# Hybrid attention encoder: in the first layer, both groups of sliding attention between differential heads 1 and 2, and an output projection that begins with their rows

## The chip, the cores and the metric

The kernel runs on one core of a Trainium2 chip. The metric is the device time of one execution in microseconds. The engines are TensorE (PE for its matmuls, PEld for its weight loads), VectorE (DVE), ScalarE (ACT), GpSimd (POOL) and SyncE (SP), which issues every DMA of this kernel.

## The reference, cut to what matters

Two sequences are encoded, a prompt of 16 + 1024 tokens and a sample of 16 + 512 tokens (the 16 are shared meta tokens). Each of two layers projects the normalised tokens, computes two kinds of attention on them, multiplies by gates, and projects back.

```python
def layer(x, ...):
    h = rmsnorm(x, pre_g)
    proj = einsum('bld,de->ble', h, w_in)            # aq ak av ag bq bk bv bg
    oa = window_gqa_attention(aq, ak, av, sink) * silu(ag)   # 8 query heads, 2 key heads
    ob = diff_attention(bq, bk, bv, lam, ...) * silu(bg)     # 4 heads, two softmaxes each
    o = einsum('ble,ed->bld', concatenate([oa, ob], -1), w_out)
    return x + rmsnorm(o, post_g)

def diff_attention(q, k, v, lam, lambda_init, subln_g):   # over all keys
    p = softmax(einsum('bqhcd,bkhcd->bhcqk', q, k) * scale)
    a = p[:, :, 0] - lam * p[:, :, 1]
    return rmsnorm(einsum('bhqk,bkhe->bqhe', a, v), subln_g) * (1 - lambda_init)
```

The sliding attention looks at a band of 128 keys to each side, at the meta tokens and at a sink.

## The kernel before, in words

A recording layer takes down every operation with what it reads and writes (so every instruction of the profile carries line 448, and tiles are told apart by name), and a planner then orders them: `Recorder.schedule` walks through a model of the engines, and each engine takes the ready operation with the lowest priority number. The number of an operation is its place in the written program, less a boost of its kind and less a base of its stage. Each engine runs its instructions in the planned order; a wait on the chip does not change it.

A layer has six attention units: four differential heads (`attn_b`, heads 0 to 3; the tuple `UNITS` calls them 0 to 3) and two groups of sliding attention (`attn_a`, groups 0 and 1; `UNITS` calls them 4 and 5). Each unit does the prompt and then the sample. The weight columns of the input projection that a unit needs (4 blocks of 128 for a differential head, 6 for group 0 with the shared keys and values, 4 for group 1) are projected while the unit before it runs:

```python
for u in range(6):
    nc.base = BASE_A[l][u]
    order[u][1](l)                                   # the attention of this unit
    if u + 1 < 6:
        es = [(e, None, 0) for e in order[u + 1][0]]  # the projection for the next
        for grp in GROUPS[1 if len(es) == 4 else 2]:
            inproj(l, *[es[i] for i in grp])
outproj(l)
```

So "fill" on PE, the dense products that stand between the pieces of an attention unit, comes from the input projection for the next unit, and for the last unit from the output projection. Tiles: `ps_d` are the two PSUM buffers of all dense products, `ps_s` the scores (one buffer), `ps_t` transposes, `ps_o` attention outputs; `pp` holds probabilities, `at` their transposes, `kk`, `qq`, `vv` the keys, queries and values, `whl` the split weights, `slot` the large activation buffers (16 of them). A product `ps_d<-slot,whl` belongs to the input projection, one with `whl,slot` (or `whl,at`, `kk`, `vv` in the place of `whl`) to the output projection. After a differential head or a sliding group, its output `og` goes to the HBM tensor `MX`, from where `load_mix` fetches it for the output projection.

The output projection has two passes over the 1024 rows of MX. `first` multiplies half `FH[l]` of them for all tokens and keeps the result; `second` multiplies the other half, chunk of tokens by chunk, and adds. Half 0 are the rows of the sliding groups, half 1 those of the differential heads. The order of the steps is written out: `b01234` is `first` for all five chunks, `f01` fetches the residual, `S01` is `second` for chunks 0 and 1, `p` are the norm and the residual, `n` the transposes for the next layer, `s4 s2 s3` the rest of `second`.

Of the kernel before, what the change touches and what calls it, by code (L numbers as in the profile page):

```python
# [55 lines left out]
GROUPS = (((0, 1), (2, 3)), ((0, 1), (2, 3)), ((0, 1), (2, 3), (4, 5)))  # L56
COMB = ((1, 1, 1, 1), (1, 1, 1, 1))
BASE = ({'f': 400, 'p': 100, 's': -100, 'S': 0, 'b': 800, 'g': -50}, {'f': 0, 'S': 400, 'l': 1000})
BASE_A = ((-200, 1500, 1500, -200, 200, 400), (0, 0, 0, 0, 1500, 300))
FH = (1, 1)  # L60
UNITS = ((0, 1, 2, 3, 4, 5), (0, 1, 2, 3, 4, 5))


def even_tiles(t0, n, m):
# [475 lines left out]
def hymba_kernel(ctx, tc, xT, xr, w_in, w_out, rope, masks, pre_g, post_g, sub_g, sink_b, sink_m, lam_in, yo):  # L540
# [244 lines left out]
    def load_w(src, pool=None, pri=0):  # L785
        nc.boost = BOOST_W + pri * 100000
        nc.extra = [after[0]] if pool and after else []
        raw = (p_p if pri or pool and after else wraw_p)([128, 1024])
        dma(raw, src)
        nc.boost = BOOST_W  # L790
        w = (pool or whl_p)([128, 2, 8, 128], F32R)
        rv = raw.rearrange("p (a c) -> p a c", a=8)
        nc.any_copy(w[:, 0], rv)
        nc.any_tt(w[:, 1], rv, f32(w[:, 0]), ALU.subtract)
        nc.extra = []
        nc.boost = 0
        return w
# [502 lines left out]
    def load_mix(l, ci, half, small=False):  # L1300
        nc.boost = BOOST_M
        his, los = [], []
        k = 2 if small else 4
        n = sum(m for _, m in OCH[ci])
        for r0 in range(4 * half, 4 * half + 4, k):
            if ci == 4:
                hi, lo = [at_p([128, 4, n], F32R) for _ in range(2)]
            else:
                hi, lo = [p_p([128, 2, CN], F32R) for _ in range(2)] if small else pair(F32R)
            o = 0  # L1310
            nc.extra = [after[0]] if small else []
            for (t0, m) in OCH[ci]:
                dma(lo[:, :, o:o + m], SC[l]["MX"][r0:r0 + k, :, t0:t0 + m].rearrange("e p t -> p e t"))
                o += m
            nc.extra = []
            nc.any_copy(hi[:, :, 0:n], f32(lo[:, :, 0:n]))
            nc.any_tt(lo[:, :, 0:n], f32(lo[:, :, 0:n]), f32(hi[:, :, 0:n]), ALU.subtract)
            his.append(hi)
            los.append(lo)
        nc.boost = 0  # L1320
        return rows(his, k), rows(los, k)
# [4 lines left out]
    def outproj(l):  # L1326
# [18 lines left out]
        def first(*cs_):  # L1345
            for ci in cs_:
                mix[ci] = load_mix(l, ci, FH[l])
                if ci < 4:
                    part[ci] = halves([128, 3, 512])
            for dp in range(4):  # L1350
                w = load_w(w_out[l, FH[l], dp])
                u, c0 = dp // 2, 256 * (dp % 2)
# [16 lines left out]
        def load(ci):  # L1369
            mix[ci, 1] = load_mix(l, ci, 1 - FH[l], ci == 3 and l > 0)  # L1370

        def second(*cs_, keep=True):
# [9 lines left out]
            def get(dp):  # L1382
                if dp not in kept:
                    w = load_w(w_out[l, 1 - FH[l], dp], (None, None, k_p, v_p)[dp] if keep else None)
                    if keep:
# [139 lines left out]
    for l in range(NL):  # L1525
        order = [units[u] for u in UNITS[l]]
        es = [(e, pool, START.get(f"w{i}", 0) if l == 0 else 0)
# [3 lines left out]
        for u in range(6):  # L1531
            nc.stream = "attn"
            nc.base = BASE_A[l][u]
            order[u][1](l)
# [63 lines left out]
```

## Time and profile before

| | |
|---|---|
| median of 3 runs | 1920.6 us (1920.0 to 1920.7) |
| the profiled execution | 1922.3 us, of which the span from first to last instruction is 1920.5 us |
| PE busy with matmuls | 1840.4 us, 96% |
| PE busy with weight loads | 1772.5 us, 92% |
| VectorE, ScalarE, GpSimd busy | 1487.8, 1028.0, 267.7 us |
| mean granted TensorE clock | 0.99 of full speed |

Busy time counts a matmul from its start to its modelled end, and matmuls overlap, so that 96% says that PE has seldom nothing at all in work, not that it runs at its peak.

### The profile page before, as it was taken

How to read it: one execution, taken by the hardware profiler on the slowest of the kernel's cores; microseconds unless marked ns; L12 is line 12 of the kernel's file. 1: busy time of each engine (PE TensorE's matmuls, PEld its weight loads, DVE VectorE, ACT ScalarE, POOL GpSimd, SP SyncE). 2: the span in 40 equal slices, each digit the busy share in tenths (PEclk: the TensorE clock that was granted, in tenths of full speed). 3: DMA queues.
4: the chain of work that ended last, by engine and by line, in shares of the span. 5: the costliest groups of instructions: out<-in, count | busy, mean ns of one | idle time of the engine just before them, and what ended most of it. 6: DMA issues, size and time to landing. Idle time of an engine off the chain costs nothing.

```text
span 1920.5 us, 35745 instructions
## 1 busy us (share of the span) xinstructions
PE 1840.4 (96%) x12400; PEld 1772.5 (92%) x12400; DVE 1487.8 (77%) x3353; ACT 1028.0 (54%) x2458; POOL 267.7 (14%) x521
## 2 busy tenths in 40 slices
PE   7999999999999998998799999999999999989998
PEld 7999999999999898898699999999999999889998
DVE  7577787888796887676987387887968859879777
ACT  8345454465554666565664255454546537658642
POOL 2011111212121110010220021111211111101101
PEclk9999999999999998999899999999999999999999
DMA  8444453634545665655454444445453475684374
GB/s 252 133 107 125 132 135 110 165 84 131 155 101 148 158 163 135 148 140 147 154 182 115 134 119 136 130 118 156 109 167 107 125 174 127 157 221 115 84 238 150
DMA packets 296498, 273.04 MB, mean 142 GB/s; under 512 B 100822, under 2 KB 259670, under 8 KB 296190
## 3 DMA queue, kind: packets, MB, share of 16 engines
q1 hardware_dynamic: 296318, 270.76, 51.0%
q8 instruction: 99, 1.62, 0.4%
q14 instruction: 81, 0.66, 0.1%
HBM read 149.19 MB, written 96.01 MB: 128 GB/s over the span
## 4 chain that ended last, share of the span: by engine, by line
PE 72%; DMA 10%; DVE 9%; issue 3%; ACT 3%; SPq 3%; POOL 1%; DVEq 0%; POOLq 0%; ACTq 0%
PE ps_d L448 44%; PE ps_s L448 10%; PE ps_o L448 9%; PE ps_t L448 9%; SPq L448 3%; DVE at L448 2%; DVE pp L448 2%; DVE slot L448 2%; DMA slot<-MX 1%; ACT pp L448 1%; DMA kk<-AK 1%; DVE whl L448 1%; DVE sm L448 1%; DVE og L448 1%; DMA wraw<-in_w_in_dram 1%
## 5 line engine op out<-in xcount | busy, mean ns | idle before, releaser
L448 PE MATMUL ps_d<-slot,whl 128*128 128x392 f32 (+2 forms) x4560 | 939.9, 346 | 16.2 <-ACT slot L448 6.9
L448 PEld LDWEIGHTS ps_d<-slot,whl 128*128 128x128 f32 x4560 | 782.6, 189 | 23.8 <-ACT slot L448 6.8
L448 PE MATMUL ps_s<-kk,qq 128*128 128x264 f32 (+9 forms) x1496 | 284.5, 319 | 21.4 <-DMA qq<-qq 6.5
L448 PE MATMUL ps_o<-at,vv 128*128 128x256 f32 (+6 forms) x1368 | 284.7, 306 | 5.8 <-DVE og L448 2.6
L448 ACT ACTIVATE at<-ps_t 128x256 fp32r<-128x256 f32 (+10 forms) x426 | 184.7, 440 | 195.9 <-PE ps_t L448 170.9
L448 DVE TENSOR_TENSOR at<-ps_t,at 128x256 fp32r<-128x256 f32 (+6 forms) x472 | 225.3, 481 | 78.7 <-ACT at L448 63.9
L448 PE MATMUL ps_d<-whl,slot 128*128 128x256 f32 x1800 | 263.7, 291 | 16.2 <-DVE slot L448 10.9
L448 ACT ACTIVATE pp<-ps_s,sm 116x1040 f32<-116x1040 f32 (+4 forms) x208 | 204.0, 981 | 131.9 <-DVE sm L448 120.7
L448 PEld LDWEIGHTS ps_s<-kk,qq 128*128 128x128 f32 (+4 forms) x1496 | 226.3, 184 | 45.2 <-issue 9.4
L448 PEld LDWEIGHTS ps_d<-whl,slot 128*128 128x128 f32 x1800 | 238.3, 194 | 22.8 <-DVE slot L448 13.3
L448 ACT ACTIVATE pp<-pp,sm 128x336 f32<-128x336 f32 (+6 forms) x347 | 207.5, 611 | 91.8 <-DVE sm L448 88.8
L448 DVE TENSOR_REDUCE sm<-ps_s 116x1 f32<-116x1040 f32 (+4 forms) x208 | 218.5, 1051 | 47.4 <-PE ps_s L448 46.0
L448 PEld LDWEIGHTS ps_o<-at,vv 128*128 128x128 f32 (+1 forms) x1368 | 213.8, 189 | 13.2 <-DVE at L448 3.7
L448 PE MATMUL ps_t<-ident,pp 128*128 128x128 f32 (+6 forms) x1280 | 206.3, 268 | 3.6 <-ACT pp L448 2.0
L448 PEld LDWEIGHTS ps_t<-ident,pp 128*128 128x128 f32 (+6 forms) x1280 | 151.1, 137 | 14.2 <-ACT pp L448 2.6
L448 POOL TENSOR_TENSOR pad<-pp,pad 128x64 fp32r<-128x64 f32 (+5 forms) x148 | 54.4, 372 | 756.4 <-ACT pad L448 410.2
L448 POOL TENSOR_TENSOR sm<-sm 128x2 f32<-128x2 f32 (+3 forms) x112 | 51.0, 456 | 466.8 <-DVE sm L448 439.3
L448 DVE CUSTOM_DVE_ANT_0 pp<-ps_s,mk,nsinks 128x336 f32<-128x336 f32 (+2 forms) x192 | 97.2, 527 | 19.5 <-PE ps_s L448 17.8
L448 POOL TENSOR_TENSOR sm<-sm,mhalf 128x1 f32<-128x1 f32 (+6 forms) x107 | 82.5, 783 | 165.5 <-DVE sm L448 162.5
L448 ACT ACTIVATE og<-ps_o 64x128 f32<-64x128 f32 (+4 forms) x248 | 66.7, 287 | 45.2 <-PE ps_o L448 29.2
L448 ACT ACTIVATE ru<-ps_d 128x392 f32<-128x392 f32 (+5 forms) x101 | 49.0, 486 | 73.3 <-PE ps_d L448 62.5
L448 DVE CAST at<-ps_t 128x256 fp32r<-128x256 f32 (+9 forms) x142 | 69.7, 491 | 18.7 <-PE ps_t L448 16.3
(157 smaller groups left out, 2115.6 us busy)
## 6 DMA issues: line engine op xcount, KB each, us to landing
wraw<-in_w_in_dram SPq DMA_DIRECT2D x46, 512.0 KB
qq<-qq SPq DMA_DIRECT2D x144, 128.0 KB
BS<-st SPq DMA_DIRECT2D x64, 196.0 KB
qq<-AQ SPq DMA_DIRECT2D x96, 128.0 KB
gl<-GT SPq DMA_DIRECT2D x72, 128.0 KB
MX<-og SPq DMA_DIRECT2D x72, 128.0 KB
slot<-MX SPq DMA_DIRECT2D x11, 768.0 KB
kk<-BS SPq DMA_DIRECT2D x8, 1040.0 KB
```

Source lines behind the costliest of these rows:

```text
L448: fn(*[_real(a) for a in args], **{k: _real(a) for k, a in kw.items()})
```

## The change

Five numbers and tuples change; no operation is added or taken away. In the first layer the units run in the order head 0, head 1, group 0, group 1, head 2, head 3 (before: heads 0 to 3, then the groups). `BASE_A` goes by place in this order: the last unit's base is 1900 in place of 400. `FH` of the first layer turns from 1 to 0: `first` takes the rows of the sliding groups, `second` those of the differential heads.

```diff
-BASE_A = ((-200, 1500, 1500, -200, 200, 400), (0, 0, 0, 0, 1500, 300))
-FH = (1, 1)
-UNITS = ((0, 1, 2, 3, 4, 5), (0, 1, 2, 3, 4, 5))
+BASE_A = ((-200, 1500, 1500, -200, 200, 1900), (0, 0, 0, 0, 1500, 300))
+FH = (0, 1)
+UNITS = ((0,1,4,5,2,3), (0,1,2,3,4,5))
```

Both programs hold 12400 matmuls. The first 1267 stand in the same order in both, and so do all from the 6511th on, counted from the start of the program; the second layer's order is the same on every engine. What differs lies between.

First place: PE in the prompt part of sliding group 1. Before, products of the output projection (`whl,slot`) stand between its pieces:

```order
L448 MATMUL ps_s<-kk,qq 128x336 x2
L448 MATMUL ps_d<-whl,slot 128x256 x18
L448 MATMUL ps_o<-at,vv 128x256 x4
L448 MATMUL ps_t<-ident,pad 80x128 x4
L448 MATMUL ps_d<-whl,slot 128x256 x6
L448 MATMUL ps_t<-ident,pp 128x128 x4
L448 MATMUL ps_d<-whl,slot 128x256 x3
L448 MATMUL ps_o<-at,vv 128x256 x2
L448 MATMUL ps_t<-ident,pp 128x128 x4
L448 MATMUL ps_o<-at,vv 128x512
```

In the changed kernel the fill of this unit is the input projection for head 2 (`slot,whl`), and in one stretch, of which the middle is shown, there is none:

```order
L448 MATMUL ps_d<-slot,whl 128x392 x9
L448 MATMUL ps_t<-ident,pp 64x128 x4
L448 MATMUL ps_s<-kk,qq 128x336 x4
L448 MATMUL ps_t<-ident,pad 80x128 x4
L448 MATMUL ps_s<-kk,qq 128x336 x2
L448 MATMUL ps_o<-at,vv 128x512 x2
L448 MATMUL ps_o<-at,vv 128x256 x5
L448 MATMUL ps_o<-at,kk 128x256
L448 MATMUL ps_o<-at,vv 128x512
L448 MATMUL ps_s<-kk,qq 128x336 x6
L448 MATMUL ps_t<-ident,pp 128x128 x8
L448 MATMUL ps_t<-ident,pp 64x128 x4
```

From the row behind the first one here on, 91 matmuls (the 3396th to the 3486th) follow each other without one into `ps_d`.

Second place: PE in the sample part of head 3. Before, its fill is the input projection for group 0:

```order
L448 MATMUL ps_s<-kk,qq 106x264 x4
L448 MATMUL ps_t<-ident,og 116x128 x2
L448 MATMUL ps_t<-ident,og 112x128
L448 MATMUL ps_d<-slot,whl 128x384 x12
L448 MATMUL ps_s<-kk,qq 106x264 x4
L448 MATMUL ps_d<-slot,whl 128x384 x3
```

In the changed kernel this is the last unit of the layer, its fill is `S01`, and between chunk 0 and chunk 1 of it stand 43 matmuls (the 5695th to the 5737th) with none, of which these are the last:

```order
L448 MATMUL ps_s<-kk,qq 106x264 x4
L448 MATMUL ps_o<-at,vv 128x212 x3
L448 MATMUL ps_t<-ident,pad 80x106 x2
L448 MATMUL ps_o<-at,vv 128x212 x4
L448 MATMUL ps_s<-kk,qq 106x264 x4
L448 MATMUL ps_t<-ident,og 106x128 x2
L448 MATMUL ps_s<-kk,qq 106x264 x4
L448 MATMUL ps_t<-ident,sm 128x106 x2
L448 MATMUL ps_s<-kk,qq 104x264 x4
L448 MATMUL ps_d<-whl,slot 128x256 x15
```

Third place: PE where the layer's last attention output is made. Before, the last `ps_o` matmul of group 1 is the 6027th, and the transposes for the next layer (`ps_t<-ident,slot`) follow soon:

```order
L448 MATMUL ps_d<-whl,slot 128x256 x3
L448 MATMUL ps_o<-at,vv 128x512
L448 MATMUL ps_d<-whl,at 80x256 x3
L448 MATMUL ps_d<-whl,slot 128x256 x57
L448 MATMUL ps_t<-ident,slot 128x128 x8
```

In the changed kernel the last `ps_o` matmul, of head 3, is the 5856th, and the rest of `S01` stands behind it:

```order
L448 MATMUL ps_o<-at,vv 128x316
L448 MATMUL ps_d<-whl,slot 128x256 x9
L448 MATMUL ps_t<-ident,og 106x128 x2
L448 MATMUL ps_t<-ident,og 104x128
L448 MATMUL ps_d<-whl,slot 128x256 x21
L448 MATMUL ps_t<-ident,sm 128x106 x2
L448 MATMUL ps_t<-ident,sm 128x104
L448 MATMUL ps_d<-whl,slot 128x256 x93
```

So the layer's attention ends 171 matmuls earlier in PE's order, and 159 matmuls, up to the 6016th, need nothing of the last group of tokens.

## Rows read from the trace of the kernel before

**Rows 1.** The page, part 1: busy us, share of the span, instructions.
```profile
PE 1840.4 (96%) x12400; PEld 1772.5 (92%) x12400; DVE 1487.8 (77%) x3353; ACT 1028.0 (54%) x2458; POOL 267.7 (14%) x521
```

**Rows 2.** Windows: heads 1 to 3, both groups, hand-over; second layer's group 0.
```profile
core 0: us, PE busy (x) PEld busy (x) DVE busy (x) ACT busy (x) POOL busy (x), PEclk, DMA share, GB/s
233.32:621.70 388.38, 384.54 (x2527) 370.86 (x2525) 319.80 (x620) 194.65 (x409) 65.06 (x140) 1.00 0.47 128
621.70:940.45 318.75, 295.14 (x2119) 280.43 (x2120) 246.79 (x731) 195.64 (x567) 33.40 (x69) 0.97 0.57 148
940.45:1021.16 80.71, 69.15 (x486) 66.48 (x485) 70.24 (x133) 51.98 (x120) 20.52 (x22) 0.92 0.52 170
1578.46:1717.01 138.55, 129.97 (x820) 121.62 (x819) 115.29 (x331) 90.93 (x254) 14.34 (x27) 1.00 0.64 164
```

**Rows 3.** The chain that ended last: start us, us, what.
```profile
975.91 13.11 PE ps_d L448 x111
...
1060.78 11.27 PE ps_d L448 x63
```

**Rows 4.** Timeline of PE: start us, us, instructions; transposes.
```profile
619.95 0.71 PE L448 MATMUL ps_t<-ident,pp 106*128 106x106 f32 x6
...
622.89 0.44 PE L448 MATMUL ps_t<-ident,pp 106*128 106x106 f32 x3
```

**Rows 5.** Groups of PE by form, 621.70 to 940.45: count, busy us, mean ns.
```profile
L448 PE MATMUL ps_d<-whl,slot 128*128 128x256 f32 x879 | 128.1, 291 | 6.8 <-DVE slot L448 4.1 <-ACT slot L448 2.7
L448 PE MATMUL ps_d<-slot,whl 128*128 128x392 f32 x183 | 41.1, 350 | 0.0
L448 PE MATMUL ps_d<-slot,whl 128*128 128x384 f32 x192 | 40.2, 343 | 0.1
L448 PE MATMUL ps_s<-kk,qq 128*128 128x336 f32 x128 | 28.4, 337 | 7.5 <-DMA qq<-qq 5.6 <-DVE sm L448 1.9
```

**Rows 6.** Windows: group 0's prompt, a fed stretch, the second layer's group 0.
```profile
621.70:722.55 100.85, 96.78 (x611) 90.70 (x611) 84.15 (x243) 64.86 (x179) 14.74 (x27) 1.00 0.66 166
...
428.10:431.50 3.40, 3.40 (x30) 3.29 (x30) 2.36 (x6) 2.74 (x6) 0.00 (x0) 1.00 0.00 0
1600.00:1640.00 40.00, 39.54 (x259) 36.73 (x258) 38.59 (x115) 32.56 (x95) 6.64 (x11) 1.00 0.51 129
```

**Rows 7.** Timeline of PE where group 0's sample part begins.
```profile
729.96 0.40 PE L448 MATMUL ps_s<-kk,qq 128*128 128x336 f32 x1
733.90 0.62 PE L448 MATMUL ps_s<-kk,qq 128*128 128x336 f32 x1 [3.54 <-DMA qq<-qq]
736.38 2.05 PE L448 MATMUL ps_s<-kk,qq 128*128 128x336 f32 x6 [1.86 <-DVE sm L448]
```

**Rows 8.** Windows before, in and after the slow clock around that stall.
```profile
724.00:731.00 7.00, 6.09 (x35) 5.37 (x33) 5.49 (x14) 2.98 (x9) 0.35 (x1) 1.00 0.95 252
731.20:741.30 10.10, 5.54 (x22) 5.15 (x23) 6.94 (x23) 7.37 (x21) 0.86 (x3) 0.50 0.73 204
741.40:748.40 7.00, 7.00 (x58) 6.78 (x57) 6.14 (x23) 4.49 (x14) 0.32 (x1) 1.00 0.25 50
```

**Rows 9.** Groups of DVE by form, 621.70 to 940.45: count, busy us, mean ns.
```profile
L448 DVE CUSTOM_DVE_ANT_0 pp<-ps_s,mk,nsinks 128x336 f32<-128x336 f32 x64 | 34.8, 560 | 3.5 <-PE ps_s L448 2.5 <-PE ps_t L448 0.5
L448 DVE TENSOR_TENSOR at<-ps_t,at 128x512 fp32r<-128x512 f32 x40 | 27.5, 687 | 9.5 <-ACT at L448 5.3 <-PE ps_o L448 2.7 <-ACT sm L448 0.8
L448 DVE SCALAR_TENSOR_TENSOR og<-ps_o,og 64x128 f32<-64x128 f32 x92 | 24.4, 284 | 8.9 <-ACT og L448 8.1
L448 DVE TENSOR_TENSOR whl<-wraw,whl 128x1024 fp32r<-128x1024 f32 x13 | 15.8, 1218 | 4.0 <-ACT whl L448 3.9
```

**Rows 10.** Timeline of PE in the hand-over to the second layer.
```profile
943.04 3.09 PE L448 MATMUL ps_d<-whl,slot 128*128 128x256 f32 x24 [0.78 <-DVE slot L448]
949.30 4.64 PE L448 MATMUL ps_d<-whl,slot 128*128 128x256 f32 x24 [3.17 <-DVE slot L448]
...
956.54 1.33 PE L448 MATMUL ps_t<-ident,slot 128*128 128x128 f32 x5 [2.28 <-ACT slot L448]
959.75 0.80 PE L448 MATMUL ps_d<-whl,slot 128*128 128x256 f32 x2 [1.88 <-ACT slot L448]
962.10 4.42 PE L448 MATMUL ps_d<-whl,slot 128*128 128x256 f32 x19 [1.55 <-DVE slot L448]
```

**Rows 11.** The chain, 850 to 1000: start us, us, what; a load of MX and its split.
```profile
862.89 6.38 DMA slot<-MX
869.29 1.49 ACT slot L448
870.81 1.77 DVE slot L448
```

## The prediction

> **What bounds the kernel now.** I read the page's busy times first, then windows by stage, then the order of the two programs. TensorE has matmuls in work for 96% of the span, VectorE works 77% of it [rows 1]. As no operation is added or taken away, only the time in which PE is not fed can change, and only between the places where the two orders are the same: from the 1386th matmul before (the first scores of head 1, at 233.32 us, the 1387th after) to the 6511th, at 1021.16 us. That is 787.84 us in three stages [rows 2]: heads 1 to 3 take 388.38, the two sliding groups 318.75, and the hand-over behind the last attention output 80.71.
>
> Busy time hides most of the loss, since a matmul that waits in the pipeline still counts. So I count what the matmuls of a stage take when PE is fed. In fed runs, 111 products of 256 columns take 13.11 us, 118 ns each, and 63 of 392 columns take 11.27 us, 179 ns each [rows 3]: at a full clock of 2.4 GHz both are columns/2.4 ns and 11 to 16 ns more, and I take 13 for all widths. A transpose adds 0.09 us ((0.71 - 0.44)/3) [rows 4]; I take 0.1. Counting each stage's forms at these prices (the largest of the sliding stage are in [rows 5]) gives:
> heads 1 to 3, 375.3 us of fed work in 388.4, a factor of 1.035; the groups, 276.8 in 318.75, 1.152; the hand-over, 62.0 in 80.7, 1.30. In the second layer, group 0 alone, with the input projection as fill, has 123.9 in 138.55, 1.118. The loss sits in the sliding stage (42 us) and in the hand-over (19 us), heads lose 13.
>
> What ends the waits there: in the groups the queries' load, late by 3.54 us and then by a chain of scores [rows 7]; in the hand-over VectorE and ScalarE, which add, norm, split and transpose for PE [rows 10] while VectorE is busy 70.24 of 80.71 us [rows 2].
>
> By the Trainium skill ("Perfetto Trace Analysis", "Identifying the Most-Contended Engine") a matmul's busy share is no good measure of how far PE is from its limit. The trace agrees: by busy time these stages have 39 us to give back (388.38 - 384.54, 318.75 - 295.14, 80.71 - 69.15), by the count of fed work 74.
>
> **The change, part by part.** Fed work of the changed order, counted in the same way, with VectorE's instructions of each part at what their forms add to its busy time in the trace (the largest in [rows 9]):
>
> Head 1, to the 2263rd matmul: 130.6 us of PE. Its fill is the projection for group 0, as head 3 had before. At 1.035: 135.2.
>
> Groups 0 and 1, 2263rd to 3966th: 256.0 us. Their fill is now wholly the input projection (products of 384 and 392 columns), no longer the products of `first`. The nearest row is the prompt part of group 0 before, 92.0 us of fed work in 100.85, 1.096 [rows 6]; second layer's group 0, where loads of MX run beside it, has 1.118, the whole stage before 1.152. I take 1.096 for all but one stretch, since here no MX loads run beside the groups: 244.5 x 1.096 = 268.0. The stretch is the 91 bare matmuls: 11.5 us of PE, beside which the order has 24.2 us of VectorE (8 of the wide mask-and-minimum instructions at 0.56, 5 wide and 3 half-wide remainders at 0.69, 10 merges of 0.28, a weight split of 1.22, the rest rotations and splits for head 2's projection, which hold the two `ps_d` buffers) and 15.6 of ScalarE. The trace of before shows no such stretch: its longest without a dense product has some 30 matmuls and lies at 428.1, where PE is busy for all of 3.40 us [rows 6]. Bounds: 11.5 if VectorE's work spreads over the neighbours, and 24.2/0.87 = 27.8 if VectorE keeps the share that it has in the hand-over. I take VectorE at the share that it reaches where it is the bound, 38.59 of 40 [rows 6]: 25.1. Sum for the groups 293.1.
>
> Heads 2 and 3, 3966th to 5857th: 245.3 us. Fill is the projection for head 3, then `first` and `S01`. VectorE has 201.4 us there, less in proportion than before, so 1.035 holds: 240.6 x 1.035 = 249.0. The rest is the second bare stretch: 4.7 us of PE, 8.7 of VectorE, because chunk 1 of `S01` needs the last prompt outputs of this very head. Bounds 4.7 and 10.0; I take 8.7/0.965 = 9.0.
>
> Behind the last attention output, 5857th to 6016th: 18.9 us of products that are ready, x 1.035 = 19.6. This is the gain of the edit to `FH` and `UNITS`: before, the last output's way through MX (6.38 us of load, 1.49 and 1.77 of splitting [rows 11]) lay half bare in front of `s2` and `s3` [rows 10].
>
> The hand-over, 6016th to 6511th: 63.2 us of PE but 76.6 of VectorE, against 71.4 counted so for before, since both halves of the residual work (`p0`, `p1`) now stand behind the attention. VectorE bounds it, so the 80.7 us of before scale: 80.7 x 76.6/71.4 = 86.6. Bounds: 76.6/0.965 = 79.4, and 86.6 + 6.4 if the load of chunk 2, which stands only 20 matmuls ahead of its use, is waited for bare.
>
> Sum: 135.2 + 268.0 + 25.1 + 249.0 + 9.0 + 19.6 + 86.6 = 792.5 against 787.8, 4.7 us more. The profiled execution took 1922.3 us, its span 1920.5, the median of the runs is 1920.6; the difference is put on the median: **1925 us**.
>
> **A second price for the bare stretches.** Around the stall at 730 the granted clock fell from 1.00 to 0.50, that is to 1.2 GHz, for 10.1 us, in which PE was busy 5.54, and came back after dense products [rows 8]. If that follows both bare stretches, up to half of 10.1 us is lost twice, 10.1 us in all. I leave it out of the sum, because in the bare stretches matmuls keep coming, where at 730 PE stood still for 3.54 and then 1.86 us [rows 7].
>
> The Trainium skill ("TensorE: Matmul & The Clock Gate", "Why this matters for your kernels") says that idle gaps between bursts of matmuls bring the lower clock back, so it speaks against this order. By it the sum would be 802.6; the trace agrees for the stall at 730, no run here shows a bare stretch of this kind.
>
> **The rivals.**
> *The groups run freely (faster).* Place: the sliding groups, in which MX loads no longer stand in front of the queries. For it: the worst wait before is such a load [rows 7], with DMA at 0.95 [rows 8]. Against it: group 0's prompt had no MX loads either and stood at 1.096, as VectorE has 84.15 of its 100.85 us [rows 6]. At the heads' 1.035 the groups cost 253.1 in place of 268.0: 1910. It decides from a factor of 1.06 down, where the sum is 9 us smaller.
> *Nothing measurable.* The work is the same and the loss only moves: VectorE takes the hand-over at 0.965 (79.4) and the bare stretches stay: 785.3, 1918.
> *The clock.* Both bare stretches halve it: 10.1 more, 1935.
>
> **How the numbers follow.** A difference of 0.2%, 3.8 us, is about what a measurement of this kernel can tell. Chances: the forecast 0.46 (own range 1920 to 1932), the groups freely 0.27, nothing measurable 0.16, the clock 0.11. Faster than 1916.8: nearly all of the second and a little of the third, 0.27. Slower than 1924.4: seven tenths of the first and all of the fourth, with a trace of the third, 0.45. Within: 0.28. With all low bounds together the sum would be about 40 us smaller, with all high ones (1.152 for the groups, bare 27.8 and 10.0, the clock, the load) 34 us larger; they will not fall together. The range is 1908 to 1940, from the rival on the faster side to just past the clock's.
>
> **What would show it.** Windows of the changed trace between its own places: head 1 in about 135 us; the groups in 293, with PE fed 1.1 times outside one stretch of some 25 us in group 1's prompt, in which VectorE is near 0.95 and `ps_d` does not appear; heads 2 and 3 in 258 with a second hole of 4 us; 20 us of pure products behind the last `ps_o`; then 87 us with VectorE above 0.85. From the 6511th matmul on, 899 us as before. It is wrong if the groups take under 280 us, if the bare stretch takes less than 17 us, if the hand-over ends in under 80, or if loads of MX hold up head 2, which I price at nothing because its queries and keys are issued well ahead.

## The result, and the profile after

The changed kernel takes 1949.05 us (median of four runs, 1947.1 to 1951.2) where the kernel before, run beside it, takes 1920.65. The ratio is 1.0133, 95% interval 1.0116 to 1.0150: slower by some 26 us (the two medians by themselves are 28 apart), on the side that was forecast, and outside the range of 1908 to 1940. The profiled execution took 1948.07 us.

The first rows are part 1 of the page, then windows of the changed kernel: the whole stretch in which the orders differ, then head 1; group 0, prompt and sample; group 1, prompt and sample; head 2; head 3; the products behind the last attention output; the hand-over; at last the two bare stretches.

```profile
PE 1853.8 (95%) x12400; PEld 1776.0 (91%) x12400; DVE 1481.2 (76%) x3345; ACT 1030.6 (53%) x2471; POOL 273.4 (14%) x516
```

```profile
core 0: us, PE busy (x) PEld busy (x) DVE busy (x) ACT busy (x) POOL busy (x), PEclk, DMA share, GB/s
234.14:1044.12 809.98, 759.10 (x5124) 718.56 (x5125) 629.87 (x1474) 442.45 (x1102) 125.65 (x226) 0.98 0.49 136
...
234.14:376.00 141.86, 134.59 (x877) 129.15 (x877) 110.30 (x220) 67.27 (x145) 24.76 (x47) 1.00 0.45 122
376.00:470.31 94.31, 89.40 (x554) 82.78 (x555) 78.75 (x236) 60.40 (x175) 15.12 (x29) 0.98 0.56 138
470.31:527.91 57.60, 52.01 (x317) 49.52 (x316) 36.01 (x120) 28.56 (x88) 3.33 (x8) 0.97 0.59 152
527.91:627.02 99.11, 87.87 (x509) 79.77 (x510) 80.89 (x238) 56.26 (x167) 10.58 (x21) 0.93 0.56 136
627.02:679.50 52.48, 51.90 (x327) 48.99 (x327) 38.40 (x122) 30.31 (x91) 5.77 (x9) 1.00 0.55 147
...
679.50:819.08 139.58, 131.87 (x914) 126.11 (x913) 107.91 (x197) 69.52 (x143) 20.25 (x43) 0.99 0.48 137
819.08:948.54 129.46, 123.80 (x979) 118.64 (x980) 93.97 (x183) 72.18 (x159) 19.50 (x40) 0.99 0.36 106
...
948.54:967.65 19.11, 19.11 (x162) 18.83 (x160) 12.02 (x28) 8.38 (x17) 4.24 (x9) 1.00 0.78 235
967.65:1044.12 76.47, 68.56 (x497) 64.78 (x496) 71.62 (x134) 49.56 (x117) 22.09 (x21) 0.98 0.48 163
...
573.79:600.52 26.73, 18.63 (x92) 15.12 (x92) 24.93 (x70) 15.98 (x46) 3.56 (x5) 0.81 0.51 122
921.95:933.21 11.26, 7.07 (x46) 5.45 (x45) 8.85 (x21) 7.40 (x19) 1.49 (x3) 0.93 0.39 120
```

The same stretch in the kernel before, then its heads 1, 2 and 3:

```profile
233.32:1021.16 787.84, 748.83 (x5128) 717.77 (x5127) 636.83 (x1482) 442.26 (x1095) 118.98 (x231) 0.98 0.52 140
233.32:363.98 130.66, 130.37 (x866) 126.89 (x864) 110.21 (x212) 62.21 (x129) 21.29 (x49) 1.00 0.47 128
363.98:487.82 123.84, 122.59 (x809) 117.64 (x808) 101.31 (x196) 65.24 (x137) 21.41 (x45) 1.00 0.47 130
487.82:621.70 133.88, 131.58 (x859) 126.33 (x857) 108.28 (x213) 67.19 (x144) 22.35 (x46) 1.00 0.47 126
```

The stretch takes 809.98 us against the 787.84 before, 22.1 more. Of the other 3.6 us by which the two profiled executions differ, 2.8 lie in the second layer, whose order is the same in both. VectorE is busy for less time than before in the stretch, PE for 10 us more, and the mean granted clock is 0.98 of full speed in both: neither more work nor a lower clock is the difference. PE's weight loads stand idle for 70.1 us of the stretch before (787.84 - 717.77) and for 91.4 after, 21 more: PE is fed worse.

The price of fed work from the prediction tells where it is. Elapsed time less fed work, in us, by stage (for the kernel before, heads 1, 2, 3 as they stood then; "tail" is all behind the last attention output, up to the 6511th matmul; matmuls are counted from 0):

| | head 1 | head 2 | head 3 | groups | tail | sum |
|---|---|---|---|---|---|---|
| before | 2.6 | 4.6 | 5.8 | 42.1 | 18.7 | 73.8 |
| changed | 11.2 | 13.3 | 10.4 | 47.6 | 13.5 | 96.0 |

Each line is one execution; e7 below, which has the changed kernel's order and nearly all of its work, gave a sum of 98.0, so a sum is good to some 2 or 3 us.

The tail gives 5 us back, the groups lose 5 more, and the three heads, the best stages of the kernel before, lose 22 more, 6.6 of it in the bare stretch of head 3 (11.26 us for 4.7 of fed work). PE's waits there are in front of the attention's own pieces. These are rows of the timelines of PE, ACT, DVE and SP in head 1 of the changed kernel (start us, us, instructions, and in brackets the idle time before them and what ended it):

```profile
258.58 0.42 PE L448 MATMUL ps_t<-ident,pp 116*128 116x116 f32 x2 [1.57 <-DVE st L448]
...
257.09 0.65 ACT L448 ACTIVATE st<-ps_t 96x256 fp32r<-96x256 f32 x2 [2.07 <-DMA AK<-st]
...
257.77 0.75 DVE L448 TENSOR_TENSOR st<-ps_t,st 96x256 fp32r<-96x256 f32 x2 [4.06 <-ACT st L448]
...
254.42 1.06 SPq L448 DMA_DIRECT2D AK<-st  x2
```

Read from the bottom: SP issues the last stores of a projected block of keys out of `st` until 255.48. There is one buffer `st`, so ScalarE's split of the next block stands until these have landed, 2.07 us; VectorE's half of that split stands behind it, 4.06 us; and the transposes of head 1's probabilities stand behind both on PE. Fill there was, but later in PE's queue. In head 2 it is the same buffer:

```profile
694.69 1.22 PE L448 MATMUL ps_s<-kk,qq 128*116 128x264 f32 x6 [1.35 <-ACT pp L448]
...
690.40 0.85 ACT L448 ACTIVATE st<-ru 128x768 fp32r<-128x768 f32 x1 [2.32 <-DMA BS<-st]
...
684.24 4.97 SPq L448 DMA_DIRECT2D BS<-st  x8
...
692.26 2.18 SPq L448 DMA_DIRECT2D BS<-st  x4
```

SP takes 4.97 us to issue the eight stores of one block; ScalarE stands for 2.32 in front of `st`, and the softmax that would free the one score buffer stands behind it. The next four stores follow at 692.26, when `st` has been filled again.

### The profile page after: what moved, and what is told of

Read it like the earlier page. It is cut to its first block, busy times and chain, and to the rows that moved or that the text cites. A ratio compares the mean times of both kernels' runs of the same rounds, so it can differ in the third digit from the quotient of the medians.

```text
span 1946.3 us, 35786 instructions
## 1 busy us (share of the span) xinstructions
PE 1853.8 (95%) x12400; PEld 1776.0 (91%) x12400; DVE 1481.2 (76%) x3345; ACT 1030.6 (53%) x2471; POOL 273.4 (14%) x516
## 5 line engine op out<-in xcount | busy, mean ns | idle before, releaser
L448 PE MATMUL ps_s<-kk,qq 128*128 128x264 f32 (+10 forms) x1496 | 287.6, 321 | 24.7 <-ACT pp L448 7.6
L448 ACT ACTIVATE at<-ps_t 128x256 fp32r<-128x256 f32 (+11 forms) x430 | 185.6, 438 | 215.6 <-PE ps_t L448 183.8
L448 PE MATMUL ps_o<-at,vv 128*128 128x256 f32 (+7 forms) x1368 | 286.1, 307 | 10.7 <-DVE at L448 6.4
L448 DVE TENSOR_TENSOR at<-ps_t,at 128x256 fp32r<-128x256 f32 (+6 forms) x472 | 225.6, 482 | 86.0 <-ACT at L448 65.5
L448 ACT ACTIVATE pp<-pp,sm 128x336 f32<-128x336 f32 (+7 forms) x344 | 205.8, 611 | 99.6 <-DVE sm L448 95.7
L448 PEld LDWEIGHTS ps_o<-at,vv 128*128 128x128 f32 (+1 forms) x1368 | 215.0, 190 | 21.8 <-DVE at L448 12.2
L448 PE MATMUL ps_t<-ident,pp 128*128 128x128 f32 (+5 forms) x1280 | 205.5, 269 | 10.2 <-ACT pp L448 3.7
L448 PEld LDWEIGHTS ps_t<-ident,pp 128*128 128x128 f32 (+5 forms) x1280 | 151.5, 137 | 22.9 <-ACT pp L448 4.5
L448 POOL TENSOR_TENSOR pad<-pp,pad 128x64 fp32r<-128x64 f32 (+4 forms) x140 | 51.9, 373 | 735.8 <-ACT pad L448 413.4
L448 POOL TENSOR_TENSOR sm<-sm 128x2 f32<-128x2 f32 (+2 forms) x112 | 52.1, 466 | 486.6 <-DVE sm L448 472.6
L448 DVE CUSTOM_DVE_ANT_0 pp<-ps_s,mk,nsinks 128x336 f32<-128x336 f32 (+2 forms) x192 | 97.5, 528 | 15.2 <-PE ps_s L448 14.1
L448 POOL TENSOR_TENSOR sm<-sm,mhalf 128x1 f32<-128x1 f32 (+7 forms) x107 | 84.8, 802 | 169.7 <-DVE sm L448 163.1
L448 ACT ACTIVATE ru<-slot 128x512 f32<-128x512 f32 (+1 forms) x82 | 51.3, 626 | 56.4 <-DVE slot L448 53.3
```

Source lines behind the costliest of these rows:

```text
L448: fn(*[_real(a) for a in args], **{k: _real(a) for k, a in kw.items()})
```

## The experiments

### Is it the bases? (e1 to e4)

Theory P says that the bases suit the old places, theory S that the order of the units costs this much whatever the bases.

```diff
 changed     BASE_A = ((-200,  1500, 1500, -200,  200, 1900),
+e1          BASE_A = ((-200,  1500, 1500, -200,  200,  400),
+e2          BASE_A = ((-200,  1500,  200,  400, 1500, 1900),
+e3          BASE_A = ((-200,  -200,  200,  400, 1500, 1900),
+e4          BASE_A = ((-200,  -200, 1500, -200,  200, 1900),
```

> The changed kernel with one edit undone: the base of the last unit is 400 again, so that S01 is not held back behind head 3. Theory P (the loss comes from bases that do not suit the units at their new places): head 3 alone changes; its bare stretch grows from 43 to 65 matmuls with 13.6 us of VectorE, which costs 3 us more than the 11.25 us of the changed kernel: 1952. Theory S (the loss comes from the order of the units, whatever the bases): the same, 1949 to 1952. This run separates the base of 1900 from the rest: were it the cause, the time would fall to about 1930.

> The changed kernel with the bases that the units had before carried to their new places: group 0 gets 200, group 1 gets 400, head 2 gets 1500 (changed kernel: 1500, -200, 200); head 1 keeps 1500, head 3 keeps 1900. Theory P: head 2 loses the 4.6 us that it lost before instead of 13.3, the bare stretch in group 1's prompt (62 matmuls in place of 91) costs 10.5 in place of 15.2, head 3's (25 in place of 43) 3 us less: 1949 - 8.7 - 4.7 - 3 = 1933. Theory S: the bare stretches alone shrink, head 2 keeps its loss of 12 us beside the splits of MX: 1949 - 7.7 = 1941.

> As the kernel with the bases by unit, and head 1, whose fill is now the projection for group 0, gets -200, the base that head 3 had with this fill before. Theory P: head 1 loses 5.9 us in place of 11.2, head 2 4.6 in place of 13.3; but the order has bare stretches of 62 matmuls in group 0's prompt (7.2 us of PE, 15.2 of VectorE, about 9 us lost) and of 99 in group 1's (26.4 of VectorE, about 1 us more than now), head 3's shrinks (3 us less): 1949 - 5.3 - 8.7 + 9 + 1 - 3 = 1942. Theory S: heads 1 and 2 keep their losses, 1949 + 9 + 1 - 3 = 1956.

> The changed kernel with the base of head 1 alone turned from 1500 to -200, so that the projection for group 0 goes ahead of the head's attention as it did in head 3 before. Theory P: head 1 loses 5.9 us in place of 11.2; the order of all later units shifts, and a bare stretch of 111 matmuls (13.3 us of PE, 18.3 of VectorE) stands in head 3 in place of the one of 43, which loses 6 to 8 us more than none: 1949 - 5.3 + 1 = 1945. Theory S: head 1 keeps 11 us of loss, 1950. Head 1's own stage decides: about 142 us of elapsed time for 135.8 of fed work by P, 147 by S.

Measured, as ratios to the kernel before beside them: e1 1.0152 (1.0124 to 1.0179), e2 1.0115 (1.0081 to 1.0148), e3 1.0145 (1.0119 to 1.0170), e4 1.0149 (1.0114 to 1.0184). None is told from the changed kernel's 1.0133. Put on 1920.65 us, e2 (1943) and e4 (1949) come out where theory S had them, e3 (1949) halfway between P and S. By stages:

| | head 1 | head 2 | head 3 | groups | tail | sum |
|---|---|---|---|---|---|---|
| e1 | 10.6 | 12.2 | 14.1 | 50.5 | 18.0 | 105.4 |
| e2 | 11.3 | 8.7 | 12.4 | 47.0 | 18.2 | 97.6 |
| e3 | 7.4 | 5.5 | 10.7 | 58.1 | 19.0 | 100.7 |
| e4 | 6.4 | 9.6 | 23.3 | 51.1 | 16.6 | 107.0 |

Stage by stage, P is right: head 1 with -200 loses 6.4 and 7.4 in place of 11.2, head 2 with 1500 loses 8.7 and 5.5 in place of 13.3. In the sum it is wrong: what a base gives to one stage is lost in another, in e1, e3 and e4 above all as longer or new bare stretches, and the tail's gain of 5 us is gone in e1, e2 and e3.

### Is it VectorE's load? (e5 to e7)

e5 and e6 cut the same 100 rotation instructions short in both kernels, at the moment at which the planned order is written out, so that no order changes; e7 cuts the split of MX.

```diff
+SMALL = tuple(range(0, 10)) + tuple(range(14, 26))
...
+def small(x):                       # on the operands of a marked VectorE instruction
+    if isinstance(x, View) and x.shape[-1] > 8:
+        return x[tuple([slice(None)] * (len(x.shape) - 1) + [slice(0, 8)])]
+    return x
...
+nc.small = l == 0 and e in SMALL    # e5, e6: rw<-ps_d and ru<-ru,rw of the rotations
+nc.small = l == 0 and half == FH[0] and ci < 4    # e7: slot<-slot in load_mix
```

> The kernel before, its order of instructions unchanged on every engine, with 100 VectorE instructions of the first layer's rotations cut to 8 columns each (rw<-ps_d and ru<-ru,rw of the projections for heads 1 to 3 and both groups; the queries and keys are then wrong beyond these columns): 45.1 us less of VectorE, 12.3 beside head 0, 11.3 beside head 1, 4.3 beside head 2, 8.6 beside head 3, 8.6 beside group 0. Theory V (VectorE's load under the fill is what the attention chain waits for): the heads here lose only 2.6 to 5.8 us each and give back 1 us each, group 0 some 4: 1921 - 7 = 1914. Theory O (what costs is where the order places chains without fill, VectorE's load is beside the point): 1918 to 1920.

> The changed kernel, its order unchanged, with the same 100 VectorE instructions cut to 8 columns: 45.1 us less of VectorE, 9.3 beside head 0, 8.6 beside head 1, 8.6 beside group 0, 9.3 beside group 1's prompt (2.5 of it in the bare stretch), 6.3 beside head 2, 3.0 beside group 1's sample. Theory V: head 1 gives back 4 of its 11.2 us of loss, the groups 5 and 6, head 2 3: 1949 - 18 = 1931, and the distance to the kernel before with the same cut falls from 28 us to 17. Theory O: at most the 2.5 us of the bare stretch and a few more, 1944, and the distance stays at 25 or more.

> The changed kernel, its order unchanged, with the four VectorE instructions of 1.75 us that split the sliding rows of MX for the output projection cut to 8 columns (6.9 us less of VectorE, all in head 2's prompt; the low parts of these rows are then wrong). Theory V: head 2's prompt, 94.9 us for 82.7 of fed work, falls by 3 to 5 us, to 91, and the time to 1945. Theory O: 0 to 1 us, 1948 to 1949.

Measured: e5 1.0011 (0.9996 to 1.0026), e6 1.0092 (1.0070 to 1.0114), e7 1.0126 (1.0104 to 1.0148). The cut took less than was counted on: the 100 instructions fell from 53 us to 17.5, 35 us in place of 45, and as instructions overlap, VectorE's busy time fell by 30 us in e5 and 31 in e6 (part 1 of their pages, against 1487.8 and 1481.2):

```profile
PE 1840.0 (96%) x12400; PEld 1773.0 (92%) x12400; DVE 1457.5 (76%) x3353; ACT 1026.5 (53%) x2458; POOL 262.5 (14%) x521
...
PE 1852.2 (95%) x12400; PEld 1776.3 (91%) x12400; DVE 1449.9 (75%) x3345; ACT 1029.8 (53%) x2471; POOL 268.8 (14%) x516
```

| | head 1 | head 2 | head 3 | groups | tail | sum |
|---|---|---|---|---|---|---|
| e5 (before, cut) | 2.8 | 4.7 | 5.5 | 44.8 | 19.2 | 76.9 |
| e6 (changed, cut) | 9.5 | 14.9 | 11.0 | 44.9 | 15.8 | 96.1 |
| e7 (changed, less split) | 10.9 | 13.4 | 10.7 | 48.9 | 14.1 | 98.0 |

The kernel before makes nothing of it. The changed kernel's ratio falls by 0.41%, 8 us, about halfway between theories O and V, and the distance from 1.33% to 1.0092/1.0011, 0.81%. But the two ratios of the changed kernel carry some 0.2% each, and the profiled execution of e6, the slowest of its four, shows no gain in the stretch: head 1 and the groups lose 4 us less, head 2, head 3 and the tail 4 more. So the worth of this cut by itself is not shown. The split of MX is no cause: head 2 loses 13.4 us without its time. And the bare stretch in group 1's prompt, out of which the cut took 3 us of VectorE (24.93 to 21.90), is 3.6 us shorter, with VectorE busy for 95% of it and a clock of 0.93 in place of 0.81; the window of e6:

```profile
571.23:594.39 23.16, 15.29 (x92) 12.41 (x91) 21.90 (x66) 15.52 (x44) 3.40 (x5) 0.93 0.52 123
```

### Another place for the groups (e8)

```diff
-UNITS = ((0,1,4,5,2,3), (0,1,2,3,4,5))
+UNITS = ((0,4,1,5,2,3), (0,1,2,3,4,5))
```

> Another order of the first layer's units, head 0, group 0, head 1, group 1, head 2, head 3, with the bases and the half of MX of the changed kernel. Group 0's fill is the projection for head 1, group 1's that for head 2, head 0's and head 1's those for the groups. Theory S (groups beside input projection, and heads behind them, cost this much wherever the groups stand): 1945 to 1960, with the groups at a factor of 1.13 or more over their fed work. If it were the place right behind head 1 that costs, or the two groups standing together, the time would come down to 1930 or less.

Measured: 1.0108 (1.0084 to 1.0132), 1945.04 us. Neither the place behind head 1 nor two groups in a row is the cause. The groups' factor is 1.166 (307.5 us for 263.8 of fed work), head 3 loses 21.1, the sum is 98.5.

### Is the old order only a well fitted point? (e9 to e12)

Theory F says that any disturbance of a fitted order costs this much. e9 and e10 add random numbers to the priorities of the first layer's units, e11 and e12 change one number each in the kernel before.

```diff
-SEED = 36
+SEED = 1
...
+nc.spread = 6 if l == 0 and u > 0 else 0                        # e9 before, e10 changed
-o.prio = o.seq - self.boost - self.base + self.rnd.random() * SPREAD
+o.prio = o.seq - self.boost - self.base + self.rnd.random() * self.spread
...
-BASE_A = ((-200, 1500, 1500, -200, 200, 400),
+BASE_A = ((-200, 1500, 1500, 1500, 200, 400),                   # e11
...
+nc.base = 40 if l == 0 and u else 0      # e12: ahead of the input projection that fills a unit
```

> The kernel before, its units in their old order, with a random 0 to 6 places added to the priority number of each operation of the first layer's units from the second on, of their fill as well: a small disturbance of the order that moves no unit and no stage. Theory S (the order of the units costs 28 us): the time stays at 1921 to 1927. Theory F (the order before is a fitted point, on which the waits happen to be short, and any other order of this planner costs about as much as the changed one): 1935 to 1950, with heads that lose some 9% in place of 3.5%.

> The changed kernel with the same random 0 to 6 places on the priority numbers of the first layer's units. The bare stretch in group 1's prompt is gone from the order; one of 121 matmuls (14.4 us of PE, 20.1 of VectorE) stands in head 3, before there were 43. Theory S and theory F both: 1945 to 1955; were the bare stretch in group 1 the main loss, the time would fall by its 15 us less 6 to 8 for the new one, to 1940.

> The kernel before with the base of head 3 turned from -200 to 1500 (the base that head 1 has, with the same fill, in the changed kernel); the order is unchanged up to the first scores of head 3. Theory S: head 3 loses 2 to 5 us more, by what head 1 of the changed kernel showed for this base, the rest stays: 1923 to 1926. Theory F: head 3 and the groups behind it lose 10 us or more beyond that: 1933 or more.

> The kernel before with 40 added to the base of the input projection that fills heads 1 to 3 and the groups, so that it goes 40 places earlier against the attention; the order of heads 1 and 2 stays as it is, that of head 3 and of the groups changes. Theory S: 1919 to 1926. Theory F: 1933 or more, with the added loss in the stages whose order changes.

Measured: e9 1.0060 (1.0045 to 1.0075), e10 1.0133 (1.0118 to 1.0148), e11 1.0051 (1.0036 to 1.0067), e12 1.0014 (0.9992 to 1.0036).

| | head 1 | head 2 | head 3 | groups | tail | sum |
|---|---|---|---|---|---|---|
| e9 (old units) | 5.5 | 8.2 | 4.1 | 37.4 | 23.8 | 79.0 |
| e11 (old units) | 2.6 | 5.6 | 10.7 | 48.4 | 18.8 | 86.1 |
| e12 (old units) | 2.7 | 4.9 | 8.6 | 42.2 | 23.5 | 81.9 |
| e10 (new units) | 14.3 | 5.8 | 14.4 | 48.4 | 18.8 | 101.7 |

Both theories have a part. Put on 1920.65 us, e9 (1932) and e11 (1930) fall between what S and F expected, e12 (1923) where S had it. A disturbed old order costs 12 us in e9 and 10 in e11; in e12 the 3 us are within the noise. So the old order looks like a good point among its neighbours, as far as three disturbances can tell. But four plans with the old units lose 73.8 to 86.1 us in the stretch, and seven with the new units (the changed kernel, e1 to e4, e10, e8) 96.0 to 107.0: the two sets do not meet. e11 is the mirror of e4: with 1500 in the place of -200, head 3 of the kernel before, whose fill is the projection for group 0, loses 10.7 us instead of 5.8, as head 1 of the changed kernel does with that base and that fill. And e10, whose order has no bare stretch in group 1's prompt, is no faster; in its place a stretch of 121 matmuls in head 3 takes 25.9 us for 14.4 of fed work.

### The one buffer st, and what is left (e13, e14, e16, e17)

```diff
+REAL = {'st': 2}
...
-tp = ctx.enter_context(tc.tile_pool(name=name, bufs=bufs))
+tp = ctx.enter_context(tc.tile_pool(name=name, bufs=REAL.get(name, bufs)))
...
-cs = const.tile([128, 2, LP], F32, name="cs")
+cs = const.tile([128, CN], F32, name="cs")
...
```

> The changed kernel, its order unchanged on every engine, with two buffers st on the chip where there was one, so that the split of a projected block need not wait until the stores of the block before have landed. (To make room the rotation table holds 392 of its 2080 columns, read for every block, so the rotations are wrong in value, and only the table's load at the start is shorter.) Theory B (ScalarE and VectorE wait in front of st with the attention queued behind them): head 1 gets back some 3 us (the waits at 257, 265 and 275), head 2 3 to 4 (at 693 and 697), the groups 2 to 4: 1949 - 9 = 1940. Theory N (what the attention waits for is spread over all links): 1946 to 1949.

> The kernel before, its order unchanged, with the same second buffer st and the same short table. Theory B: 1 to 3 us less than before, since its heads lose 13 us in all and most of its waits for stores lie beside fill: 1918 to 1920, and the distance between the two kernels shrinks from 26 to 28 us to about 19. Theory N: no change in either, and the distance stays.

> The changed kernel, its order unchanged, with both edits at once: two buffers st (and the short rotation table), and the 100 rotation instructions of VectorE cut to 8 columns. If the two causes are separate, their gains add: 0.41% from the rotations and 0.75% from the buffer, 1.0133 - 0.0116 = 1.0017 of the kernel before, 1927 to 1929. If they are one cause (VectorE late because it stands before st), the second edit adds nothing: 1.006.

> The kernel before with both edits: from the buffer 0.53% less, from the rotations nothing (0.11% more alone, within the interval): 0.9947 to 0.995. The distance between the two orders would then be 0.7%, some 13 us, if the causes are separate, and 1.1% if they are one; what is left of it belongs to the order itself, to its bare stretches first.

Measured: e13 1.0058 (1.0036 to 1.0079), e14 0.9947 (0.9924 to 0.9970), e16 1.0000 (0.9983 to 1.0017), e17 0.9954 (0.9935 to 0.9972).

| | head 1 | head 2 | head 3 | groups | tail | sum |
|---|---|---|---|---|---|---|
| e13 (changed, two st) | 6.5 | 9.7 | 10.1 | 49.4 | 14.6 | 90.3 |
| e14 (before, two st) | 2.5 | 2.7 | 4.9 | 41.0 | 20.9 | 72.0 |
| e16 (changed, two st, cut) | 5.9 | 11.6 | 10.4 | 40.0 | 14.5 | 82.4 |
| e17 (before, two st, cut) | 2.5 | 4.4 | 5.5 | 40.1 | 20.4 | 72.9 |

At the two places shown above the wait is gone. The rows of e13 that answer to them, PE, ACT and DVE in head 1, then PE and ACT in head 2:

```profile
253.86 0.36 PE L449 MATMUL ps_t<-ident,pp 116*128 116x116 f32 x2
...
251.94 0.64 ACT L449 ACTIVATE st<-ps_t 96x256 fp32r<-96x256 f32 x2
...
252.61 0.75 DVE L449 TENSOR_TENSOR st<-ps_t,st 96x256 fp32r<-96x256 f32 x2 [1.88 <-ACT st L449]
...
687.21 1.10 PE L449 MATMUL ps_s<-kk,qq 128*116 128x264 f32 x6
...
682.28 0.84 ACT L449 ACTIVATE st<-ru 128x768 fp32r<-128x768 f32 x1
```

ScalarE's split now follows the softmax ahead of it at once, and PE's transposes and scores carry no bracket. Head 1 gets 4.7 us back, head 2 3.6, as theory B had it; the groups, from which it expected 2 to 4, get nothing. But the kernel before gains too, 0.53%, five times what I expected, and where is not shown: its stretch is 1.8 us shorter, and the second layer, which has the same buffer, 3.7 us in e14 but not in e17 (891.8 us against 891.9). Nor does any run have the short table alone, so that some of either kernel's gain may be the table's. The distance is 1.0058/0.9947, 1.12%, still.

With both cuts it is 1.0000/0.9954, 0.46% or 9 us: 0.52 points are gone by the rotations alone, 0.21 by the buffer alone, 0.87 by both. Each ratio carries some 0.2%, so that the single shares are rough, and the buffer's share of the distance is not resolved by the times alone; what both do together is clear of the noise. The 0.46% is nearer to the 0.7% expected of two separate causes than to the 1.1% of one. What is left of the distance in the stretch, 82.4 - 72.9 = 9.5 us, lies in the heads: 27.9 against 12.4, with the tail 6 us better. So of the 22 us that the heads had lost more, 15 stay with both cuts; in this profile the groups gave back as much (47.6 to 40.0) as the heads (34.9 to 27.9).

### The bare stretch in head 3 (e15)

```diff
-O0 = "b01234 f01 S01 g l2 p0 l3 p1 s4 s2 n0 s3 f4 p4 f2 p2 n1 f3 p3 n2 n3"
+O0 = "b01234 f01 S0 S1 g l2 p0 l3 p1 s4 s2 n0 s3 f4 p4 f2 p2 n1 f3 p3 n2 n3"
```

> The changed kernel with S0 S1 in the place of S01 in the first layer's steps: the products of chunk 0 with the heads' rows no longer alternate with those of chunk 1, which need the last prompt outputs of head 3, and the bare stretch of 43 matmuls in head 3 is gone from the order. Four weight blocks more are loaded and split (1.06 us of ScalarE and 1.22 of VectorE each). If the bare stretch costs what head 3's sample lost, 6 us come back: 1943. If its cost only moves on to the hand-over, where VectorE has 5 us more to do: 1949 to 1952.

Measured: 1.0152 (1.0126 to 1.0178). Head 3 loses 7.7 us in place of 10.4 and the tail 18.2 in place of 13.5; together they take 225.6 us, against 225.0 in the changed kernel. The cost moved on to the hand-over, the second of the two outcomes, and the bare stretch in group 1 is still there (26.6 us); another 8 us of this profile lie in the second layer, 902.7 us against 894.7.

## Why the prediction was wrong

Its steps, against the stages of the profiled execution:

| step | forecast | measured |
|---|---|---|
| head 1, 130.6 x 1.035 | 135.2 | 141.86, factor 1.086 |
| groups without the bare stretch, 244.5 x 1.096 | 268.0 | 276.8, factor 1.132 |
| bare stretch in group 1 | 25.1 | 26.73 |
| heads 2 and 3 without theirs, 240.6 x 1.035 | 249.0 | 257.8, factor 1.071 |
| bare stretch in head 3 | 9.0 | 11.26 |
| behind the last attention output | 19.6 | 19.11 |
| hand-over | 86.6 | 76.47 |
| sum | 792.5 | 809.98 |

**The step that failed** is "At 1.035", for head 1 and again for heads 2 and 3: the factor of a stage was carried over from the row of the kernel before as if it belonged to the kind of unit. It belongs to a unit, its fill and its base together (e4, e11), and to where a planned order happens to put a piece of attention behind a split. In place of 1.035 the changed kernel's heads had 1.086, 1.106 and 1.088. Twelve planned orders show heads that lose from 2.6 to 23.3 us on 108 to 138 us of fed work. With the same fault in the groups' 1.096, these three terms are 24.3 us short; the hand-over, 10 us too dear, hid part of that. The cause of the heads' loss is shown only in part: with a second `st` (e13, e16) they lose 7 to 9 us less, of the 22. Of the distance between the two kernels, 1.33%, the buffer and the cut rotations together take 0.87 points away. The rest stays open.

**Bare stretches.** Both were found where the order has them, 1.6 and 2.3 us longer than forecast, the second past its bound of 10.0. VectorE is busy 24.93 of 26.73 us, and PE waits for its merges (timeline of PE):

```profile
579.17 0.39 PE L448 MATMUL ps_o<-at,vv 128*128 128x256 f32 x1 [1.91 <-DVE at L448]
...
595.84 0.60 PE L448 MATMUL ps_t<-ident,pp 128*64 128x128 f32 x4 [2.31 <-DVE at L448]
```

Together the two take 38.0 us for 16.2 of fed work. The 21.8 us lost in them are as much as the whole growth of the loss, 73.8 to 96.0: outside them the changed kernel loses about what the kernel before does, the heads 15 us more, the groups 10 and the tail 5 less. That does not show that they are the cause. e10, which lacks the first, loses as much in its groups as the order that has it, and e15, which lacks the second, is no faster. But every planned order with the new units has a stretch of 62 matmuls or more without a dense product, none with the old units one of over 29, and no run has the new units without any: this rival is not refuted.

**The hand-over** was 10 us too dear. I scaled 80.7 by VectorE's work, but the 80.7 held 19 us of waits with a clock of 0.92 [rows 2, 10]; in the changed one the clock is at 0.98 and VectorE busy for 71.62 of 76.47 us, where I had counted 76.6 of work, so that it ends 3 us under even the low bound (79.4). Behind the last attention output the edit to `FH` and `UNITS` does what was said of it; the whole tail loses 5 us less than before.

**The clock** as a rival: in the bare stretch it was granted 0.81 of full speed, so part of it ran at the lower level of 1.2 GHz, behind pauses of PE as those shown. The Trainium skill ("TensorE: Matmul & The Clock Gate", "Why this matters for your kernels") says that idle gaps between bursts bring the lower clock back. The trace agrees in kind, but the pauses here, 1.91 and 2.31 us, are shorter than the gaps that the section speaks of; the measurement decides. Over the whole stretch, however, the mean is 0.98 before and after: before, the clock fell in other places [rows 8, 2]. It is not the difference.

**"The groups run freely"** is refuted: without MX loads ahead of the queries, group 0's prompt and sample still wait for loads (2.49 us at 482.33, one of several), and stand at 1.16. Nor was the row behind 1.096 free of such loads: before, SP issued four loads of MX from 709.68 us on, in the last 13 us of that window [rows 6].

**The sign and the chances.** Slower had 0.45, the largest, on the ground of the bare stretches and the hand-over. The bare stretches cost a little more than was said (38.0 us against 34.1); the hand-over got cheaper, and the heads, which outside their bare stretch had no part in that ground, lost 15 us more there. So the right sign is in part luck. The high bounds together gave 34 us more than the sum; none of them was for the heads, where 1.035 had no bound at all, though rows 2 showed factors up to 1.30 for other stages.

What stays open: what part of the distance the bare stretches hold, and the last 9 us of it, most of it in heads 2 and 3, whose waits with both cuts are for `pp` and `at`. Whether they are bound to this order of units, or only to the plans tried, the runs do not tell. Nor does any run undo the edit to `FH` alone. A second `st` takes 6.1 KB a partition and has no room beside the whole rotation table; a smaller form was not tried.

## What to carry to other kernels

In these runs a factor over fed work was a property of one planned order, not of a kind of stage; when an order is changed, bound it from the best to the worst stage of the profile, not by the nearest one. A fitted order may have gained on its neighbours already (10 and 12 us in two of three trials here), and a new one gives this up before it gains anything. And look for single buffers that are freed by a store: each one puts a DMA's landing in front of everything queued on the engines that fill it, and here a second one, with a shorter table load, went with 0.53% less time in one kernel and 0.75% in the other.

## What had not been expected of the hardware

A pause of 2.49 us on PE, and one of 0.90 soon behind it, were followed within some 2 us by a stretch at the lower level of 1.2 GHz in which PE had no pause (timeline of PE, then windows of the changed kernel):

```profile
482.33 0.39 PE L448 MATMUL ps_s<-kk,qq 128*128 128x336 f32 x1 [2.49 <-DMA qq<-qq]
483.62 0.63 PE L448 MATMUL ps_d<-slot,whl 128*128 128x384 f32 x2 [0.90 <-DVE ru L448]
...
485.89 1.88 PE L448 MATMUL ps_s<-kk,qq 128*128 128x336 f32 x6
487.57 0.71 PE L448 MATMUL ps_d<-slot,whl 128*128 128x384 f32 x2
```

```profile
484.60:487.90 3.30, 3.30 (x13) 3.30 (x13) 1.97 (x10) 2.75 (x10) 0.64 (x2) 0.50 0.61 178
```

From the first of the six products of 336 columns to the product behind them it is 1.68 us (485.89 to 487.57), 280 ns each, where the price of fed work at the full clock is 153. So nearly half of this time is lost, and it is the pauses' second price. Issuing takes SP's own time: eight stores of one block held it for 4.97 us, some 0.6 each. And 30 us of VectorE, 2% of its busy time, removed from a kernel that keeps it busy for 77% of the span, changed nothing there that the times resolve.
